# Decay rows stored by unit in device memory, and the Fourier stage's tiles moved to the other side of the on-chip memory

## The chip, the core and the metric

The kernel runs on one core of a Trainium2 chip. The core has a matrix engine (TensorE, PE in the profile; PEld is its weight load), three engines for elementwise work (VectorE or DVE, ScalarE or ACT, GpSimd or POOL), a queue engine (SyncE or SP) that issues nearly all transfers of this kernel, and 16 DMA engines that carry them between device memory (DRAM) and the on-chip memories SBUF and PSUM. Each engine works through its own instructions in order. The metric is the device time of one execution in microseconds; three runs of the kernel before took 3012.8, 3020.76 and 3021.59 us, so the median is 3020.76 us.

## The reference: what is computed

One encoder layer over two sequences (1024 and 2048 tokens of width 1024):

```python
proj = rms_norm(h, norm_w) @ w_in          # z_f, u_f, z_s, xbc, dt for all branches
y_f  = einsum(real(fft2(u_f)), w_fmix) * silu(z_f)            # Fourier branch, 512 wide
x, B, C = silu(conv5(xbc));  dt = softplus(dt_raw + bias)     # SSD branch, 24 heads of 64
# per head and direction, chunks of 128 tokens, a_cs = cumsum(dt * A) inside a chunk:
y_diag = (C B^T * exp(where(mask, a_cs[l] - a_cs[s], -inf))) @ (x * dt)
state  = scan over chunks;   y_off = (C state) * exp(a_cs)
y_s  = rms_norm((y_fwd + y_bwd + D * x) * silu(z_s))
h    = h + concat(y_f, y_s) @ w_out
h    = rms_norm(h + (p @ w_ple_in) * sigmoid(h @ w_ple_gate))
```

The SSD branch runs forward and backward over the tokens; d is the direction (0 forward, 1 backward).

## The kernel before: tiling, stages and order

**Blocks.** The tokens are worked off in three blocks of 1024: P (the short sequence), S1 and S2 (the halves of the long one). Every fp32 product is three matmuls on split operands (high times high, high times low, low times high).

**First stage: projection and SSD.** For each block the normed and turned rows stand in SBUF as `uh`/`ul` (lines 254 to 268). A job (class `Job`) loads 128 columns of `w_in` (`weights_in`, line 182, tile `wr`), splits them (`wh` on ACT, line 189; `wl` on POOL, line 190) and multiplies them in three pieces (line 361). Between those pieces the SSD work of the running units is put. A unit is two heads; there are twelve per block. The order of this stage is written out by hand: `pre` and `post` hang each step of a unit to a numbered slot, and every engine gets its instructions in that order.

**Decay rows.** Once per block `dt_rows` makes `rows` (the cumulated decays `a_cs`, one row of 128 tokens for each of 64 columns and 8 chunks; columns 0 to 23 hold the forward heads, 32 to 55 the backward ones) and `erow`, their exponentials. `dt_out` stores them to `ROWd` and `EXPd`, laid out by chunk, then column, then token. A unit then reads them back spread over the partitions: `rows_in` (line 540, tile `R`, four pairs of chunks, two directions each) for the masked part, `decays` (line 635, tile `er`, two groups of four chunks, two directions and two heads each) for the states' part. `rows_cut` masks `R` on POOL (line 548), `rows_exp` takes the exponential on ACT (558), `rows_joined` adds the two directions and multiplies with `cb` on DVE (563, 564), `diag` multiplies on PE (575) and adds the skip on DVE (580). `weighted` (POOL, 587) and `states` (PE 607, DVE 614 and 618) carry the states; `across` (PE 649, DVE 652 and 653) adds their part with `er`; `gated` (POOL, 658) applies the gate and `out` (line 667) stores `y` to `Yd`.

**Fourier stage.** Behind the first stage, and no longer ordered by hand but by a scheduler that works on a modelled timeline, come eight steps (two sequences, four tiles of channels). Each loads `U` (line 913), folds it into even and odd parts on DVE and POOL (982 to 992), multiplies with small matrices on PE (`pm` 972, `pe` 1000, `pq` 1017), splits (`qh` ACT 1020, `ql` DVE 1021), multiplies with the tables `th`/`tl` (1026) and combines into `yv` (DVE 1030 to 1040, POOL 1044). The tables are loaded through `traw` (928) and split on ACT and DVE (929, 930).

**Products.** Then come the output products (line 1102) in two passes and the last pass with the gated embedding (1292).

**Pools.** SBUF and PSUM are given out as two stacks, one growing from each side. The tiles of the first stage lie in the order `uh`/`ul`, weights, raw tiles, constants, unit tiles, and last the SSD's small tiles with `R`, `er` and `y`. Before, the Fourier stage's inputs, folds and first two tables (`fp`, `ft_`) lie on the right and its outputs and other tables (`fq`, `fc`) on the left, as do `ox`, `wa`, `wb` of the products; in PSUM `pm`/`pe`, `pq` and the first results lie on the right. Tiles of a later pool wait for the tiles of an earlier one whose memory they take over (`reuse_waits="tile"`).

Of the kernel before, what the change touches and what calls it, by code (L numbers as in the profile page):

```python
# [56 lines left out]
def tile_hybrid_encoder(ctx: ExitStack, tc: tile.TileContext, a):  # L57
# [14 lines left out]
    ROWd = [dram.tile([NCH, 64, P], F32, name=f"ROWd{i}") for i in range(3)]  # L72
    EXPd = [dram.tile([NCH, 64, P], F32, name=f"EXPd{i}") for i in range(3)]
# [21 lines left out]
    def bcast_rows(src, n):  # L95
        return src.partition_broadcast(n)
# [5 lines left out]
    with ExitStack() as ph:  # L102
# [63 lines left out]
        def dt_weights_in():  # L166
            wdr = sp.tile([P, KT, 64], F32, tag="R1", bufs=3, name="wdr")
# [70 lines left out]
        def x_normed(b, i, xn):  # L238

            xt, n = xn  # L240
            if b["n"] == "P":
                junk = sp.tile([P, DM], BF16, tag="R0", bufs=3, name="junk")
# [191 lines left out]

        def dt_softplus(B, part):
# [12 lines left out]
            dtm = sp.tile([P, NCH, 64], F32, tag="R1", bufs=3, name="dtm")  # L448
            dmx = sp.tile([P, NCH, 64], F32, tag="R0", bufs=3, name="dmx")
            de = sp.tile([P, NCH, 64], F32, tag="R0", bufs=3, name="de")  # L450
            dz = sp.tile([P, NCH, 64], F32, tag="R1", bufs=3, name="dz")
# [73 lines left out]
        class Unit:  # L525
# [8 lines left out]
            def rows_in(self, p):  # L534
                B, u, cc = self.B, self.u, 2 * p
                self.R[p] = []
                for d in range(2):
                    hc = 32 * d + 2 * u
                    R = sp.tile([P, 2, 2, P], F32, tag=f"R{d}", bufs=3, name=f"R{d}")
                    nc.sync.dma_start(  # L540
                        R.rearrange("p c h l -> p c (h l)"),
                        bcast_rows(ROWd[B.bi][cc:cc + 2, hc:hc + 2, :].rearrange("c h l -> c (h l)"), P))
                    self.R[p].append(R)

            def rows_cut(self, p):
                for d, R in enumerate(self.R[p]):
                    sgn = 1 if d == 0 else -1
                    G.affine_select(  # L548
                        out=R.rearrange("p c h l -> p (c h) l"), in_=R.rearrange("p c h l -> p (c h) l"),
                        pattern=[[0, 4], [sgn, P]], compare_op=ALU.is_ge, fill=NEG, base=0,  # L550
                        channel_multiplier=-sgn)
# [834 lines left out]
```

## Time and profile before

| what | value |
|---|---|
| runs | 3012.8, 3020.76, 3021.59 us |
| the profiled execution's own time | 3021.5 us |
| its span (first to last instruction) | 3019.7 us |
| mean granted TensorE clock | 0.974 |
| busy share PE, PEld, DVE, ACT, POOL | 94%, 85%, 73%, 46%, 49% |
| bytes moved, mean rate | 440.54 MB, 146 GB/s |

The first stage runs to about 1960 us, the Fourier stage from there to about 2100 us, the products to the end. In the profile a line of a timeline gives the start, the time, the engine, the source line, the operation and its tiles, and in square brackets how long the engine had been idle and for what; a line of the stretches gives, for each engine, its busy time and number of instructions, then the granted clock, the busy share of the DMA engines and the rate in GB/s; a line of the waits gives the engine and line that waited, what it waited for, the total, the number of times and the longest.

### The profile page before, as it was taken

The page shows a single profiled execution, that of the slowest core. Times are in us where ns is not written, and L with a number is a line of the kernel's source. Part 1 is how long each engine was busy: PE and PEld are TensorE (multiplying, and loading weights), DVE is VectorE, ACT ScalarE, POOL GpSimd, SP SyncE. Part 2 cuts the span into 40 slices and gives each one's busy share as a digit, 9 for nine tenths or more (in the row PEclk, how much of TensorE's full clock was granted, in tenths as well). Part 3 has the DMA queues.
Part 4 walks back from the last instruction along what each step waited for, and adds up shares of the span by engine and source line. Part 5 has one row for each costly group of instructions (what it writes and reads, how often), then busy time and mean ns, then how long its engine had stood idle before and what let it go on. Part 6 is the DMA issues. An engine that isn't in the chain of part 4 may idle for free. (4 is left out here: it accounts for less than half of the span.)

```text
span 3019.7 us, 47067 instructions
## 1 busy us (share of the span) xinstructions
PE 2831.3 (94%) x17252; PEld 2570.1 (85%) x17252; DVE 2217.9 (73%) x3412; ACT 1389.5 (46%) x2980; POOL 1488.2 (49%) x1114
## 2 busy tenths in 40 slices
PE   6999999989999989989999999978899899989998
PEld 6899999989999889989999999867677677768887
DVE  3687777666778667666868777687989888866665
ACT  4544545434545454434544444334433533355554
POOL 1255646432567566542556564455787688610000
PEclk9999999999999999999999999979999999999999
DMA  3388877872789779853677687666553654352221
GB/s 97 77 130 160 167 156 170 139 142 78 143 163 171 164 188 155 160 153 74 122 164 144 154 160 137 127 217 235 168 181 130 231 166 147 126 199 91 94 85 69
DMA packets 454578, 440.54 MB, mean 146 GB/s; under 512 B 24384, under 2 KB 405444, under 8 KB 450508
## 3 DMA queue, kind: packets, MB, share of 16 engines
q1 hardware_dynamic: 454060, 436.50, 61.5%
q8 instruction: 136, 2.23, 0.3%
q14 instruction: 94, 0.77, 0.1%
q10 hardware_dynamic: 288, 1.05, 0.1%
HBM read 328.41 MB, written 110.10 MB: 145 GB/s over the span
## 5 line engine op out<-in xcount | busy, mean ns | idle before, releaser
L361 PE MATMUL ps<-uh,wh 128*128 128x342 f32 (+1 forms) x2880 | 962.3, 334 | 11.7 <-ACT uh L267 8.5
L361 PE MATMUL ps<-ul,wh 128*128 128x342 f32 (+1 forms) x2880 | 926.1, 322 | 2.5 <-DVE ul L268 2.5
L361 PE MATMUL ps<-uh,wl 128*128 128x342 f32 (+1 forms) x2880 | 927.2, 322 | 0.9 <-POOL wl L190 0.9
L190 POOL TENSOR_TENSOR wl<-wr,wh 128x1024 fp32r<-128x1024 f32 x120 | 298.9, 2491 | 712.2 <-ACT wh L189 698.6
L361 PEld LDWEIGHTS ps<-uh,wh 128*128 128x128 f32 x2880 | 551.2, 191 | 35.3 <-issue 16.0
L361 PEld LDWEIGHTS ps<-ul,wh 128*128 128x128 f32 x2880 | 553.6, 192 | 4.2 <-DVE ul L268 3.5
L361 PEld LDWEIGHTS ps<-uh,wl 128*128 128x128 f32 x2880 | 549.8, 191 | 1.7 <-POOL wl L190 1.6
L558 ACT ACTIVATE R<-R,lb 128x128 f32<-128x128 f32 x1152 | 356.1, 391 | 89.5 <-POOL R L548 88.0
L548 POOL TENSOR_SCALAR_AFFINE_SELECT R<-R 128x512 f32<-128x512 f32 x288 | 270.4, 954 | 117.0 <-DMA R<-ROWd 113.0
L618 DVE SCALAR_TENSOR_TENSOR H<-H,cd,pst 128x64 f32<-128x64 f32 x888 | 182.7, 275 | 92.6 <-PE pst L607 90.4
L587 POOL TENSOR_TENSOR xw<-xm,wd 128x512 f32<-128x512 f32 x144 | 188.6, 1319 | 74.1 <-ACT xm L423 62.5
L1102 PE MATMUL X<-whP,ah 128*128 128x512 f32 x480 | 195.2, 407 | 7.8 <-ACT pu L1111 5.4
L402 DVE SCALAR_TENSOR_TENSOR xT<-raw,cvt,xT 128x1024 f32<-128x1024 f32 x144 | 197.3, 1370 | 2.6
L367 ACT COPY raw<-ps 128x342 f32<-128x342 f32 x180 | 78.3, 438 | 252.9 <-PE ps L361 247.9
L1102 PE MATMUL X<-whP,al 128*128 128x512 f32 x480 | 192.1, 400 | 2.1 <-DVE al L1073 2.1
L1102 PE MATMUL X<-wlP,ah 128*128 128x512 f32 x480 | 193.1, 402 | 0.5 <-DVE wlP L861 0.5
L1214 POOL TENSOR_TENSOR ht<-ht,pu 128x512 f32<-128x512 f32 x96 | 155.4, 1627 | 62.9 <-ACT pu L1111 39.9
L607 PE MATMUL pst<-xw,Bm 128*128 128x128 f32 x1056 | 146.4, 281 | 28.6 <-POOL xw L587 28.6
L607 PEld LDWEIGHTS pst<-xw,Bm 128*128 128x128 f32 x1056 | 137.5, 195 | 33.8 <-POOL xw L587 33.6
L563 DVE TENSOR_TENSOR R<-R,R 128x512 f32<-128x512 f32 x144 | 141.3, 981 | 31.4 <-ACT R L558 28.8
L1073 DVE TENSOR_TENSOR al<-s,ah 128x512 fp32r<-128x512 f32 x144 | 143.6, 1019 | 20.2 <-ACT ah L1072 20.0
L653 DVE TENSOR_TENSOR y<-y,yt 128x512 f32<-128x512 f32 (+1 forms) x144 | 154.6, 1073 | 4.9
(264 smaller groups left out, 5665.4 us busy)
## 6 DMA issues: line engine op xcount, KB each, us to landing
R<-ROWd SPq DMA_DIRECT2D x288, 256.0 KB
wr<-in_w_in SPq DMA_DIRECT2D x120, 512.0 KB
er<-EXPd SPq DMA_DIRECT2D x288, 128.0 KB
Hd<-ht SPq DMA_DIRECT2D x48, 512.0 KB
ht<-Hd SPq DMA_DIRECT2D x48, 512.0 KB
y<-Yd SPq DMA_DIRECT2D x46, 512.0 KB
wlP<-WSd SPq DMA_DIRECT2D x21, 1024.0 KB
Yd<-y SPq DMA_DIRECT2D x72, 256.0 KB
```

Of the source, the lines that this page charges most:

```text
L190: G.tensor_tensor(wl, raw, wh.bitcast(F32), op=ALU.subtract)
L361: T.matmul(ps[:, :n], lhsT=wt[:, kt, :], rhs=ut[:, kt, :n], start=(i == 0), stop=(i == 3 * KT - 1))
L402: V.scalar_tensor_tensor(dst, raw[:, k:k + TB], cvt[:, 20 * k + ct:20 * k + ct + 1], dst, op0=ALU.mult, op1=ALU.add)
L548: G.affine_select(out=R.rearrange("p c h l -> p (c h) l"), in_=R.rearrange("p c h l -> p (c h) l"), pattern=[[0, 4], [sgn, P]], compare_op ...
L558: S.activation(R[:, c, h, :], R[:, c, h, :], AF.Exp, bias=self.B.lb[:, 2 * p + c, hc + h:hc + h + 1])
L587: G.tensor_tensor(xw, self.xm[c4].rearrange("p c (h e) -> p c h e", h=2), col(self.B.wd[:, c4:c4 + 4, hc:hc + 2]).broadcast_to([P, 4, 2, 6 ...
L607: T.matmul(pst[:, c, :], lhsT=B.Bm[self.g][:, c4 + c, :], rhs=xw[:, c, :, :].rearrange("p h e -> p (h e)"), start=True, stop=True)
L618: V.scalar_tensor_tensor(dst[:, e], H[d][:, cc, e], B.cd[:, cc, hc + h:hc + h + 1], pst[:, c, e], op0=ALU.mult, op1=ALU.add)
L653: V.tensor_tensor(y[:, cr], y[:, cr], t[:, cr], op=ALU.add)
L1073: V.tensor_tensor(al, src, ah.bitcast(F32), op=ALU.subtract)
L1102: T.matmul(ps, lhsT=at[:, k, :], rhs=wt[:, k, :], start=(first and i == 0), stop=(i == 11), skip_group_check=not first)
L1214: return lambda t: G.tensor_tensor(h, h, t, op=ALU.add)
```

## The change

**Decay rows.** `ROWd` becomes [pair of chunks, head, direction, 2 x 128] and `EXPd` [group of four chunks, head, direction, 4 x 128]. A unit's rows of one pair, both heads and both directions, stand behind each other, and so do one head's rows of one group in both directions. `rows_in` issues one transfer in place of two, into one tile `R` that holds both directions; `decays` issues two in place of four. `dt_out` stores in four transfers in place of two. The steps on POOL, ACT, DVE and PE work on the same numbers with other strides. The tiles `R0` and `R1` (three buffers each) become one tag `R` of twice the size with three buffers, which the constants and the softplus use too.

**Pools.** All pools behind the first stage change sides; in PSUM `pm`/`pe` and `pq` come to the left and all results `pr` to the right.

```diff
-    ROWd = [dram.tile([NCH, 64, P], F32, name=f"ROWd{i}") for i in range(3)]
-    EXPd = [dram.tile([NCH, 64, P], F32, name=f"EXPd{i}") for i in range(3)]
+    ROWd = [dram.tile([4, 24, 2, 2 * P], F32, name=f"ROWd{i}") for i in range(3)]
+    EXPd = [dram.tile([2, 24, 2, 4 * P], F32, name=f"EXPd{i}") for i in range(3)]
...
+        def pair_of(name):
+            t = sp.tile([P, 2, NCH, 64], F32, tag="R", bufs=3, name=name)
+            return t[:, 0], t[:, 1]
...
-            nc.sync.dma_start(ROWd[B.bi].rearrange("c h l -> h c l"), B.rows)
-            nc.sync.dma_start(EXPd[B.bi].rearrange("c h l -> h c l"), B.erow)
+            for d in range(2):
+                for kept, src, n in ((ROWd, B.rows, 2), (EXPd, B.erow, 4)):
+                    nc.sync.dma_start(kept[B.bi][:, :, d, :].rearrange("p h x -> h p x"),
+                                      src[32 * d:32 * d + 24].rearrange("h (p c) l -> h p (c l)", c=n))
...
             def rows_in(self, p):
-                B, u, cc = self.B, self.u, 2 * p
-                self.R[p] = []
-                for d in range(2):
-                    hc = 32 * d + 2 * u
-                    R = sp.tile([P, 2, 2, P], F32, tag=f"R{d}", bufs=3, name=f"R{d}")
-                    nc.sync.dma_start(
-                        R.rearrange("p c h l -> p c (h l)"),
-                        bcast_rows(ROWd[B.bi][cc:cc + 2, hc:hc + 2, :].rearrange("c h l -> c (h l)"), P))
-                    self.R[p].append(R)
+                R = sp.tile([P, 2, 2, 2, P], F32, tag="R", bufs=3, name="R")
+                nc.sync.dma_start(
+                    R.rearrange("p h d c l -> p (h d c l)"),
+                    bcast_rows(ROWd[self.B.bi][p, 2 * self.u:2 * self.u + 2].rearrange("h d x -> (h d x)"), P))
+                self.R[p] = R
...
-                V.tensor_tensor(E[0], E[0],
-                                self.B.cb[self.g][:, 2 * p:2 * p + 2, :].unsqueeze(2).broadcast_to([P, 2, 2, P]),
-                                op=ALU.mult)
+                cb = self.B.cb[self.g][:, 2 * p:2 * p + 2, :].rearrange("p c l -> p (c l)")
+                V.tensor_tensor(E[0], E[0], cb.unsqueeze(1).broadcast_to([P, 2, 2 * P]), op=ALU.mult)
...
-            def decays(self, d, c4):
+            def decays(self, c4):
-                hc = 32 * d + 2 * self.u
-                er = sp.tile([P, 4, P], F32, tag=f"er{d}", bufs=2, name=f"er{d}")
+                er = sp.tile([P, 2, 4, P], F32, tag="er", bufs=2, name="er")
                 for h in range(2):
-                    nc.sync.dma_start(er[h * 64:h * 64 + 64],
-                                      bcast_rows(EXPd[self.B.bi][c4:c4 + 4, hc + h, :], 64))
-                self.er[d, c4] = er
+                    nc.sync.dma_start(
+                        er[h * 64:h * 64 + 64].rearrange("p d c l -> p (d c l)"),
+                        bcast_rows(EXPd[self.B.bi][c4 // 4, 2 * self.u + h].rearrange("d x -> (d x)"), 64))
+                self.er[c4] = er
...
-    ox = ctx.enter_context(tc.tile_pool(name="ox", bufs=1, **L_))
-    wa = ctx.enter_context(tc.tile_pool(name="wa", bufs=1, **L_))
+    ox = ctx.enter_context(tc.tile_pool(name="ox", bufs=1, **R_))
+    wa = ctx.enter_context(tc.tile_pool(name="wa", bufs=1, **R_))
...
-        ft_ = ph.enter_context(tc.tile_pool(name="ft_", bufs=1, **R_))
-        fp = ph.enter_context(tc.tile_pool(name="fp", bufs=2, **R_))
-        fq = ph.enter_context(tc.tile_pool(name="fq", bufs=2, **L_))
-        fc = ph.enter_context(tc.tile_pool(name="fc", bufs=1, **L_))
+        ft_ = ph.enter_context(tc.tile_pool(name="ft_", bufs=1, **L_))
+        fp = ph.enter_context(tc.tile_pool(name="fp", bufs=2, **L_))
+        fc = ph.enter_context(tc.tile_pool(name="fc", bufs=1, **R_))
+        fq = ph.enter_context(tc.tile_pool(name="fq", bufs=2, **R_))
+        fpl = ph.enter_context(tc.tile_pool(name="fpl", bufs=1, space=PSUM, **L_))
         fpr = ph.enter_context(tc.tile_pool(name="fpr", bufs=1, space=PSUM, **R_))
-        fpl = ph.enter_context(tc.tile_pool(name="fpl", bufs=1, space=PSUM, **L_))
...
-            pm = fpr.tile([P, 2, P], F32, tag="pm", name="pm")
+            pm = fpl.tile([P, 2, P], F32, tag="pm", name="pm")
...
-                pr = (fpr if i < 2 else fpl).tile([P, 512], F32, tag="pr", bufs=2 + i // 2, name="pr")
+                pr = fpr.tile([P, 512], F32, tag=f"pr{i // 2}", bufs=2 + i // 2, name="pr")
...
-    mp = ctx.enter_context(tc.tile_pool(name="mp", bufs=1, **R_))
+    mp = ctx.enter_context(tc.tile_pool(name="mp", bufs=1, **L_))
...
-                    q4 = ctx.enter_context(tc.tile_pool(name="q4", bufs=1, **R_))
+                    q4 = ctx.enter_context(tc.tile_pool(name="q4", bufs=1, **L_))
```

**How instructions move.** The lines of the changed kernel are one or two lower than the same lines before. A number behind a name counts tiles and says nothing here; what stands behind the arrow is read.

SP in the first unit of block P, before: loads of the rows `R` and `er` between those of the weights `wr`.

```order
L182 DMA wr<-in_w_in 128x8x128
L540 DMA R_1112<-ROWd_67 128x2x256
L540 DMA R_1114<-ROWd_67 128x2x256
L182 DMA wr<-in_w_in 128x8x128
L540 DMA R_1225<-ROWd_67 128x2x256
L540 DMA R_1227<-ROWd_67 128x2x256
L635 DMA er_1272<-EXPd_70 64x4x128 x2
L635 DMA er_1275<-EXPd_70 64x4x128 x2
L182 DMA wr<-in_w_in 128x8x128
L635 DMA er_1386<-EXPd_70 64x4x128 x2
L635 DMA er_1389<-EXPd_70 64x4x128 x2
```

The same place in the changed kernel.

```order
L182 DMA wr<-in_w_in 128x8x128
L540 DMA R<-ROWd_67 128x1024
L182 DMA wr<-in_w_in 128x8x128
L540 DMA R<-ROWd_67 128x1024
L633 DMA er<-EXPd_70 64x1024 x2
L182 DMA wr<-in_w_in 128x8x128
L633 DMA er<-EXPd_70 64x1024 x2
```

Nothing changes its place; each pair of `R` has become one transfer and each four of `er` two, with 1024 numbers in a row.

SP at the end of the first stage, before: the last unit's loads of `er`, the stores of the last projections (`UFd`, `ZFd`), of a state (`HBd`) and of the last unit's output (`Yd`), and then the Fourier stage's first inputs (`bd`, `U`, `wbd`).

```order
L667 DMA Yd_62<-y 128x512
L635 DMA er_20600<-EXPd_72 64x4x128 x2
L635 DMA er_20603<-EXPd_72 64x4x128 x2
L288 DMA UFd_64<-ft 128x1024
L635 DMA er_20679<-EXPd_72 64x4x128 x2
L635 DMA er_20682<-EXPd_72 64x4x128 x2
L979 DMA Z<-ZFd_65 128x1024
L288 DMA ZFd_66<-ft 128x1024
L288 DMA HBd<-hend 128x128
L667 DMA Yd_62<-y 128x512 x2
L900 DMA bd<-in_bdft 128x2x128
L913 DMA U<-UFd_63 128x1024
```

The same place in the changed kernel.

```order
L666 DMA Yd_62<-y 128x512
L633 DMA er<-EXPd_72 64x1024 x2
L288 DMA UFd_64<-ft 128x1024
L633 DMA er<-EXPd_72 64x1024 x2
L898 DMA bd<-in_bdft 128x2x128
L911 DMA U<-UFd_63 128x1024
L905 DMA wbd<-in_w_fmix 64x4x64
L288 DMA ZFd_66<-ft 128x1024
L905 DMA wbd<-in_w_fmix 64x4x64
L926 DMA traw<-in_tabs 128x512 x2
L911 DMA U<-UFd_63 128x1024 x2
L926 DMA traw<-in_tabs 128x512 x2
```

`bd` and `U` now stand right behind the last `er`; the two stores of `Yd` have gone behind the loads of `U` and `traw`, and the first `Z` too.

PE at the same place, before: the last unit's masked part (`pd`) and states' part (`po`), then the Fourier stage's first products.

```order
L575 MATMUL pd<-R_20447,xm 64x128 x4
L649 MATMUL po_20702<-CT,H_20584 128x128 x4
L649 MATMUL po_20710<-CT,H_20523 128x128 x4
L575 MATMUL pd<-R_20554,xm 64x128 x4
L649 MATMUL po_20725<-CT,H_20584 128x128 x3
L649 MATMUL po_20732<-CT,H_20523 128x128 x4
L972 MATMUL pm<-wbd,bd 128x128 x2
L1000 MATMUL pe<-edge,mt 128x2
```

The same place in the changed kernel.

```order
L574 MATMUL pd<-R,xm 64x128 x4
L970 MATMUL pm<-wbd,bd 128x128 x2
L998 MATMUL pe<-edge,mt 128x2
L1015 MATMUL pq<-mt,fold_20330 128x128 x2
L1015 MATMUL pq<-mt,fold_20331 128x128 x2
L648 MATMUL po_20198<-CT,H_20086 128x128 x4
L648 MATMUL po_20206<-CT,H_20027 128x128 x4
L574 MATMUL pd<-R,xm 64x128 x4
L648 MATMUL po_20221<-CT,H_20086 128x128 x3
L648 MATMUL po_20228<-CT,H_20027 128x128 x4
```

The first step's `pm`, `pe` and `pq` now stand ahead of the last unit's `po` and its last `pd`. DVE and POOL are mixed in the same way: DVE's first fold of `U` (line 980 of the changed kernel) stands between the addition and the multiplication of the last unit's third `R`.

More of the change, by code (lines that the diff above doesn't have):

```diff
@@ L534, in rows_in, with rows_cut @@
             def rows_in(self, p):
[L535 to L546 removed]
+                R = sp.tile([P, 2, 2, 2, P], F32, tag="R", bufs=3, name="R")
[3 more added lines that the diff above has]
+                self.R[p] = R
+            def rows_cut(self, p):
+                for d in range(2):
+                    R = self.R[p][:, :, d]
                     sgn = 1 if d == 0 else -1
[L548 to L551, printed above, removed]
+                    G.affine_select(out=R, in_=R, pattern=[[0, 2], [0, 2], [sgn, P]], compare_op=ALU.is_ge, fill=NEG,
+                                    base=0, channel_multiplier=-sgn)
             def rows_exp(self, p):
[L554 removed]
+                R = self.R[p]
+                for d in range(2):
                     hc = 32 * d + 2 * self.u
@@ L576, in diag @@
                                  lhsT=self.xm[c4][:, c2 + c, h * 64:h * 64 + 64],
-                                 rhs=self.R[p][0][:, c, h, :], start=True, stop=True)
+                                 rhs=self.R[p][:, h, 0, c, :], start=True, stop=True)
                 if p % 2:
@@ L690, in plan @@
                 post(s0 + 12, self.states, 1, 0)
-                for d in (1, 0):
-                    pre(s0 + 11, self.decays, d, 0)
-                    pre(s0 + 13, self.decays, d, 4)
+                pre(s0 + 11, self.decays, 0)
+                pre(s0 + 13, self.decays, 4)
                 for p in range(4):
```

31 lines of the change are left out of this document (14 added, 17 removed).

## The prediction

> **What bounds the kernel now.** I read the engines' busy shares first, then the stretches by stage, then PE's waits and the timeline around the longest. The busy shares and five stretches (start to end, busy time and instructions of each engine, granted clock, DMA share, GB/s):
>
> ```profile
> PE 2831.3 (94%) x17252; PEld 2570.1 (85%) x17252; DVE 2217.9 (73%) x3412; ACT 1389.5 (46%) x2980; POOL 1488.2 (49%) x1114
> ...
> 30.00:1950.00 1920.00, 1843.08 (x12778) 1779.54 (x12777) 1372.71 (x2320) 905.15 (x2044) 992.48 (x764) 0.98 0.72 142
> 1950.00:1975.50 25.50, 7.35 (x54) 6.45 (x54) 12.85 (x34) 1.50 (x5) 3.68 (x4) 0.70 0.66 173
> 1975.50:2060.00 84.50, 69.84 (x349) 60.59 (x349) 81.21 (x158) 38.59 (x97) 51.21 (x30) 0.84 0.67 235
> 2060.00:2100.00 40.00, 40.00 (x195) 33.75 (x196) 22.40 (x35) 14.12 (x24) 18.94 (x13) 0.92 0.43 155
> ```
>
> PE sets the time, so only what PE loses can be won. In the first stage (30 to 1950 us) it is idle for 1920 - 1843.08 = 76.9 us and granted 0.98 of its clock, another 38 us at most (0.02 x 1920, partly the same idle time). In the 25.5 us behind it PE works 7.35 us: a hole between two stages. Then DVE is the bound (81.21 of 84.5 us) with PE at 0.84 of its clock, and then PE again (40 of 40 us). Who kept PE, POOL, DVE and ACT waiting (total us, times, longest):
>
> ```profile
> PE pst L607 <- POOL xw L587: 28.6, 18, 6.9
> PE pt L264 <- DVE xt L250: 20.8, 5, 12.2
> PE pm L972 <- DVE Ue L985: 15.8, 1, 15.8
> PE pt L264 <- DVE H L618: 13.6, 4, 5.6
> ...
> POOL R L548 <- DMA R<-ROWd: 113.0, 57, 4.7
> ...
> DVE xt L250 <- DMA xt<-in_x_sample: 27.9, 4, 12.4
> ...
> ACT wh L189 <- DMA wr<-in_w_in: 56.2, 31, 6.2
> ```
>
> The 12.2 us is the kernel's start, which nothing here touches. The 15.8 us is the hole. Behind the others stand transfers. The timeline of all engines shows two such stalls, at the start of block S1 and inside it:
>
> ```profile
> 634.92 11.02 SPq L122 DMA_DIRECT2D xt<-in_x_sample  x1
> 646.52 1.28 DVE L250 SCALAR_TENSOR_TENSOR xt<-xt,ss,nwb 114x1024 f32<-114x1024 f32 x1 [12.42 <-DMA xt<-in_x_sample]
> 647.96 1.82 PE L264 MATMUL pt<-ident,xt 114*128 114x114 f32 x8 [5.72 <-DVE xt L250]
> ...
> 1118.24 2.35 POOL L190 TENSOR_TENSOR wl<-wr,wh 128x1024 fp32r<-128x1024 f32 x1 [4.47 <-ACT wh L189]
> 1125.24 2.08 PE L607 MATMUL pst<-xw,Bm 128*128 128x128 f32 x8 [6.88 <-POOL xw L587]
> ```
>
> In the first DVE stands 12.42 us for `xt`, whose issue on SP took 11.02 us, and PE loses 5.72 us. In the second POOL is late with `wl`, because `wh` and before it the load `wr` were late, and `xw` queues behind. The hole itself:
>
> ```profile
> 1940.04 0.87 SPq L540 DMA_DIRECT2D R<-ROWd  x2
> 1946.13 7.45 SPq L635 DMA_DIRECT2D er<-EXPd  x4
> 1961.61 7.56 SPq L667 DMA_DIRECT2D Yd<-y  x2
> 1969.74 0.46 SPq L913 DMA_DIRECT2D U<-UFd  x1
> ...
> 1948.24 0.32 PE L361 MATMUL ps<-uh,wl 128*128 128x342 f32 x1
> 1949.82 0.63 POOL L548 TENSOR_SCALAR_AFFINE_SELECT R<-R 128x512 f32<-128x512 f32 x1 [3.21 <-DMA R<-ROWd]
> ...
> 1964.83 0.56 DVE L652 TENSOR_TENSOR yt<-po,er 128x384 f32<-128x384 f32 x1 [3.94 <-DMA er<-EXPd]
> 1967.57 1.26 POOL L658 TENSOR_TENSOR y<-y,zT 128x512 f32<-128x512 f32 x1 [5.98 <-DVE y L653]
> 1974.67 0.69 DVE L982 TENSOR_TENSOR Ue<-U 128x511 f32<-128x511 f32 x1 [3.65 <-DMA U<-UFd]
> 1975.50 1.20 PE L972 MATMUL pm<-wbd,bd 128*128 128x128 f32 x4 [15.76 <-DVE Ue L985]
> ```
>
> The last four `er` loads take SP 7.45 us to issue and land at 1964.83; `y` is gated at 1967.57; SP holds its queue 7.56 us for the stores of `y`; only then `U` is issued, 21 us after the last projection (1948.24), and PE starts 15.76 us after it ran dry.
>
> **The change part by part.** *Instructions.* PE, ACT, DVE and POOL keep their counts and element counts. The steps concerned (us in all, mean ns):
>
> ```profile
> L558 ACT ACTIVATE R<-R,lb 128x128 f32<-128x128 f32 x1152 | 356.1, 391 | 89.5 <-POOL R L548 88.0 <-DMA wr<-in_w_in 1.4
> L548 POOL TENSOR_SCALAR_AFFINE_SELECT R<-R 128x512 f32<-128x512 f32 x288 | 270.4, 954 | 117.0 <-DMA R<-ROWd 113.0 <-DVE yt L652 4.0
> L563 DVE TENSOR_TENSOR R<-R,R 128x512 f32<-128x512 f32 x144 | 141.3, 981 | 31.4 <-ACT R L558 28.8 <-issue 2.4
> ```
>
> Their operands become two runs of 256 numbers instead of one of 512. No row has that form; the masks in the row above already ran as four rows of 128, so I take 0. If each of the 288 masks and 288 additions and multiplications on DVE cost 50 ns more, that is 14 us on engines with 928 and 547 us of idle time in the first stage: still under 2 us on PE.
>
> *Transfers.* 288 loads `R` become 144, 288 loads `er` become 144; six stores are added (4 for 2 in each of three blocks), under the projections of the first unit. How the DMA engines carry short and long runs (the queue's totals, the two tables' loads, and three stretches of 10 us):
>
> ```profile
> q1 hardware_dynamic: 454060, 436.50, 61.5%
> R<-ROWd SPq DMA_DIRECT2D x288, 256.0 KB
> er<-EXPd SPq DMA_DIRECT2D x288, 128.0 KB
> 630.00:640.00 10.00, 10.00 (x74) 9.62 (x73) 3.98 (x5) 3.94 (x11) 4.16 (x6) 1.00 1.03 76
> 640.00:650.00 10.00, 4.28 (x26) 3.89 (x25) 3.35 (x5) 1.75 (x4) 1.04 (x2) 0.81 0.67 177
> 2040.00:2050.00 10.00, 8.72 (x50) 7.23 (x48) 10.00 (x17) 8.30 (x16) 2.80 (x2) 1.00 1.02 399
> ```
>
> A load `R` reads runs of two heads by 128 numbers, 1 KB, so 256 runs each; a load `er` runs of 512 B, also 256. That is 2 x 73728 of the queue's 454060 packets. Afterwards both read runs of 4 KB: 144 x 128 + 144 x 64 = 27648. The bytes stay. If time goes with bytes, the share stays 61.5%; if it goes with packets, it falls to 61.5% x 334/454 = 45%. The nearest rows: the crowded stretch from 630 us carries 76 GB/s with the engines full, the Fourier stage's, whose loads have long runs, 399 GB/s. The first stage's mean, 142 GB/s at 0.72, is 197 GB/s at a full share. The two tables' 113 MB (288 x 384 KB) take 574 us of full engines at 197 GB/s and 284 us at 399: 290 us less, 9.6% of the span. So I take a share of about 50%, between the two bounds.
>
> What PE wins: the waits above that a late transfer can end are, without the start, 5.7 + 13.6 + 28.6 = 48 us, with up to 38 us of clock behind all 77. Bounds: 0 and 86 us. I take three quarters of the waits at the block starts (`xt` late: 14 us), a quarter of the waits for `xw` (POOL also waits there for other things: 8 us) and a sixth of the clock (6 us): **28 us**.
>
> *The hole.* `U` can be issued when the last projection has read `uh` and `ul` (1948.24 + 0.32) and lands 4.93 us later, as before (1969.74 to 1974.67): 1953.5. In the changed order nothing but the `er` loads and two stores stands ahead of it on SP. DVE then fills its idle time in the hole, 25.5 - 12.85 = 12.65 us, less some 2 us in which the first folds pass from engine to engine: 10.6 us. PE, which starts earlier and without the long pause behind which its clock was 0.84, gives about 3 us more in the stretch to 2100, where it is the bound at clock 0.92. Sum **14 us**. Bound above: DVE's work from 1950 to 2100 is 12.85 + 81.21 + 22.4 = 116.5 of 150 us, so 33 us. Bound below: 0, if the mixing costs what it wins: DVE's first fold waits for `U` ahead of the third `R`'s multiplication, `pd` queues behind that on PE, and PE's `po` behind `pe` and `pq`. With `U` at 1953.5 that holds `pd` until about 1955 and PE idles some 4 us; each us by which `U` comes later is a us lost.
>
> The stores `Yd` and the load `Z`, now behind `U` on SP, are read in the products and at the end of a Fourier step; the Fourier stage covers them. Should `Z` be late, POOL's gate of `yv` is late next.
>
> Against the profiled execution's own 3021.5 us: 3021.5 - 28 - 14 = 2979.5; the median lies 0.7 us under it, so **2979 us**.
>
> **The rivals.** (1) *Run length does not matter.* For it stands the stretch from 640 us above: 177 GB/s at 0.67 is 264 at a full share, with the same tables' loads in it, so the 76 is an extreme, and what keeps 399 away may be the spreading of one row over many partitions, which stays. Against it stands the first stage's mean, half of 399. Then the first stage keeps its stalls: 3021 - 14 = 3007. The Trainium skill has a rule to that effect: "DMA: Bandwidth & Descriptors", Specifications, calls 512 B the smallest transfer at line rate. By it both tables' runs are long enough already, and the sum would be 3007. The rows above do not bear it out for this traffic.
>
> (2) *The hole's time comes back.* DVE bounds the Fourier stage, and its order there is another; if folds and table splits now hold `pr` up, only the first stage's gain and 2 us stay: 2991.
>
> (3) *Slower: the first mask waits for both directions.* Today the two halves of `R` land apart: the last pair was issued at 1940.04 and the second mask still waited 3.21 us at 1949.82. In one transfer the first mask gets nothing before the whole has landed, and POOL's `xw` queues behind it. POOL's 113 us of waiting for `R` go with PE's 28.6 us for `xw`, a quarter. If every one of 144 first masks came x us later than now, PE would lose 36x us. Without the gain of 28 us and with that of the hole, it is slower by more than 9 us from x = 0.64; at x = 1 it gives 3021 - 14 + 36 = 3043. Against it: fewer packets should bring the whole sooner than the second half came.
>
> (4) *It does little.* The stalls stem from SP's order and POOL's load rather than from the engines' load, and the hole is half closed: about 3014.
>
> **How the numbers follow.** Forecast 62%, rival (1) 14%, (2) 12%, (3) 5%, (4) 7%. The forecast's own range is 2958 to 2999: 10 to 45 us from the first stage, 8 to 25 from the hole, seldom both at an end. With (1) and (2) the range is **2956 to 3008**. A change of 0.3% (9 us) can be told from none: faster by more than that are the forecast, (2) and most of (1), 0.87; the same (4) and the rest of (1), 0.08; slower (3), 0.05.
>
> **What would show it.** In the profile of the changed kernel: POOL's wait for `R` well under 113 us and the queue's share near 50%; no 12 us wait of DVE for `xt`; PE idle in the first stage some 50 us instead of 77 at clock 0.99. `U` issued before 1950 us less the gain so far, and no PE gap over 5 us between the last projection and `pm`. Wrong: a share near 61% with the same waits (rival 1), DVE idle in the Fourier stage and PE waiting for `ql` and folds (2), POOL's wait for `R` above 113 us (3).

## The result

The changed kernel takes 2939.93 us (median, 2936.23 to 2940.29) against 3018.89 us of the kernel before (3012.8 to 3021.59, with a fourth run beside the three named at the start): a ratio of 0.974, 95% interval 0.972 to 0.976. It is some 79 us faster; forecast were 42, and 2939.9 lies below the range of 2956 to 3008 us.

The profile page of the changed kernel, its busy shares and its largest DMA queue (packets, MB, share of the 16 engines):

```profile
PE 2803.6 (95%) x17252; PEld 2549.2 (87%) x17252; DVE 2218.9 (76%) x3412; ACT 1384.3 (47%) x2980; POOL 1513.5 (52%) x1114
...
q1 hardware_dynamic: 327484, 436.08, 47.0%
```

Nearly the same bytes (436.08 MB, 436.50 before) kept the queue busy for 47.0% of 2937.6 us instead of 61.5% of 3019.7 us, which is 1381 instead of 1857 us of full engines. To place the gain I cut both executions at the same two points, the end of the last projection on PE and the start of the first output product. The kernel before by these stretches (start to end and length; busy time of PE, PEld, DVE, ACT, POOL; clock, DMA share, GB/s):

```profile
30.00:1948.56 1918.56, 1841.64 (x12764) 1778.39 (x12763) 1371.80 (x2316) 903.75 (x2039) 992.30 (x763) 0.98 0.72 142
1948.56:2097.40 148.84, 116.04 (x601) 99.88 (x600) 115.08 (x225) 54.01 (x128) 72.54 (x45) 0.84 0.60 204
2097.40:3019.70 922.30, 860.86 (x3837) 680.44 (x3836) 719.41 (x849) 415.86 (x787) 417.94 (x298) 0.98 0.42 144
```

The changed kernel by the same view:

```profile
30.00:1868.95 1838.95, 1813.63 (x12757) 1755.52 (x12756) 1377.61 (x2320) 896.32 (x2038) 1019.89 (x765) 1.00 0.49 149
1868.95:2007.30 138.35, 112.64 (x602) 97.45 (x601) 113.89 (x223) 56.10 (x130) 71.04 (x44) 0.88 0.60 209
2007.30:2937.60 930.30, 864.56 (x3837) 684.97 (x3835) 716.17 (x848) 415.77 (x785) 417.28 (x298) 0.98 0.42 143
```

The first stage is 79.6 us shorter (1918.56 - 1838.95). PE's idle time there fell from 76.9 to 25.3 us, which is 51.6 us, and nearly the same matmuls (12757 records for 12764) took 28.0 us less busy time, at clock 1.00 instead of 0.98. The stretch up to the first product lost 10.5 us, the products grew by 8.0. So nearly all of the net gain, 79.6 of 82.1 us, is the first stage's.

PE's, POOL's and ACT's waits in the changed kernel (total us, times, longest):

```profile
POOL R L549 <- DMA R<-ROWd: 6.8, 3, 3.9
...
PE pt L264 <- DVE xt L250: 14.5, 3, 12.2
...
ACT wh L189 <- DMA wr<-in_w_in: 4.7, 2, 4.2
PE pst L606 <- POOL xw L586: 3.4, 9, 0.9
...
PE pt L264 <- DVE H L617: 2.6, 2, 2.0
```

POOL waits 6.8 us for `R` instead of 113.0, ACT 4.7 us for `wr` instead of 56.2, PE 3.4 us for `xw` instead of 28.6. The 14.5 us for `xt` all lie in the first 30 us, the kernel's start. The loads of `R` now leave SP almost at once. How long SP held the issue of a load `R`, kernel before (shortest/median/longest in ns, first and last start in us):

```profile
L540 SPq DMA_DIRECT2D R<-ROWd x288: 359/546/7210, 119.2 to 1940.5; - x144
```

The changed kernel:

```profile
L540 SPq DMA_DIRECT2D R<-ROWd x144: 319/327/836, 118.9 to 1860.6; - x144
```

Its timeline at the start of block S1, where SP's issue of `xt` had taken 11.02 us, and through the transition:

```profile
603.60 0.69 SPq L122 DMA_DIRECT2D xt<-in_x_sample  x2
...
1868.80 0.32 PE L361 MATMUL ps<-uh,wl 128*128 128x342 f32 x1
...
1869.14 0.33 SPq L911 DMA_DIRECT2D U<-UFd  x1
...
1873.59 0.69 DVE L980 TENSOR_TENSOR Ue<-U 128x511 f32<-128x511 f32 x1 [1.02 <-DMA U<-UFd]
...
1876.21 1.12 PE L574 MATMUL pd<-R,xm 128*64 128x128 f32 x8 [4.75 <-DVE H L617]
...
1877.26 1.23 PE L970 MATMUL pm<-wbd,bd 128*128 128x128 f32 x4
...
1893.55 1.22 PE L970 MATMUL pm<-wbd,bd 128*128 128x128 f32 x4 [6.91 <-DVE ed L1000]
```

`U` is issued when the last projection has read its operands, and `pm` stands 8.5 us behind that projection instead of 27.3. A new gap of 6.91 us follows ahead of the second step's `pm`.

### The profile page after: what moved, and what is told of

It is laid out like the page before. It is cut to its first block, busy times and chain, and to the rows that moved or that the text cites. A ratio compares the mean times of both kernels' runs of the same rounds, so it can differ in the third digit from the quotient of the medians.

```text
span 2937.6 us, 46491 instructions
## 1 busy us (share of the span) xinstructions
PE 2803.6 (95%) x17252; PEld 2549.2 (87%) x17252; DVE 2218.9 (76%) x3412; ACT 1384.3 (47%) x2980; POOL 1513.5 (52%) x1114
## 3 DMA queue, kind: packets, MB, share of 16 engines
q1 hardware_dynamic: 327484, 436.08, 47.0%
## 5 line engine op out<-in xcount | busy, mean ns | idle before, releaser
L361 PEld LDWEIGHTS ps<-uh,wh 128*128 128x128 f32 x2880 | 544.4, 189 | 36.3 <-issue 15.6
L361 PEld LDWEIGHTS ps<-ul,wh 128*128 128x128 f32 x2880 | 547.3, 190 | 4.2 <-DVE ul L268 3.5
L361 PEld LDWEIGHTS ps<-uh,wl 128*128 128x128 f32 x2880 | 543.7, 189 | 1.2 <-POOL wl L190 0.9
L1100 PE MATMUL X<-whP,ah 128*128 128x512 f32 x480 | 196.3, 409 | 15.9 <-ACT pu L1109 12.4
L1212 POOL TENSOR_TENSOR ht<-ht,pu 128x512 f32<-128x512 f32 x96 | 155.7, 1631 | 64.4 <-ACT pu L1109 49.9
L652 DVE TENSOR_TENSOR y<-y,yt 128x512 f32<-128x512 f32 (+1 forms) x144 | 161.3, 1120 | 4.9
L565 DVE TENSOR_TENSOR R<-R,cb 128x512 f32<-128x512 f32 x144 | 149.7, 1040 | 4.9
L272 ACT ACTIVATE zT<-ps 128x342 f32<-128x342 f32 (+1 forms) x108 | 49.1, 454 | 220.7 <-PE ps L361 220.4
L651 DVE TENSOR_TENSOR yt<-po,er 128x512 f32<-128x512 f32 (+1 forms) x144 | 91.2, 633 | 74.9 <-PE po L648 66.9
```

What stands on the lines that cost most here:

```text
L361: T.matmul(ps[:, :n], lhsT=wt[:, kt, :], rhs=ut[:, kt, :n], start=(i == 0), stop=(i == 3 * KT - 1))
L565: V.tensor_tensor(E[0], E[0], cb.unsqueeze(1).broadcast_to([P, 2, 2 * P]), op=ALU.mult)
L652: V.tensor_tensor(y[:, cr], y[:, cr], t[:, cr], op=ALU.add)
L1100: T.matmul(ps, lhsT=at[:, k, :], rhs=wt[:, k, :], start=(first and i == 0), stop=(i == 11), skip_group_check=not first)
L1212: return lambda t: G.tensor_tensor(h, h, t, op=ALU.add)
```

## The experiments

My theory was the prediction's: long runs, so fewer packets. The rivals were the number of transfers, and that the pools' sides had brought the gain. Ratios are against runs of the kernel before beside it on the same chip (medians from 3012.6 to 3018.65 us).

**The two halves of the change.** The first kernel has the rows alone, the second the pools' sides alone.

```diff
 # e1_rows: the changed kernel, and for all pools behind the first stage
-    ox = ctx.enter_context(tc.tile_pool(name="ox", bufs=1, **R_))
+    ox = ctx.enter_context(tc.tile_pool(name="ox", bufs=1, **L_))
...
 # e2_sides: the kernel before, and for all those pools
-    ox = ctx.enter_context(tc.tile_pool(name="ox", bufs=1, **L_))
+    ox = ctx.enter_context(tc.tile_pool(name="ox", bufs=1, **R_))
```

> The decay rows alone; the pools behind the first stage stay on their old sides. In the changed kernel the last projection on PE starts 79 us earlier than before (1868.8 for 1948.2 us), the stretch from there to the first output product is 10 us shorter and the products are 8 us longer. Theory A (the first stage's gain is all of it and comes from the rows): last projection near 1869 us, time 2935 to 2950 us. Theory B (the gain needs the other sides, since the Fourier stage's inputs come in earlier): last projection later than 1900 us, time above 2970 us. If the 10 us and the 8 us belong to the sides, the stretch behind the last projection is about 149 us and the products about 922 us, as before.

> The pools' sides alone; the decay rows as before. Theory A: the first stage is as before (last projection near 1948 us), time 3005 to 3020 us; by the prediction's term for the hole (14 us) it is 3005, by what the two traces show behind the last projection (10 us less, 8 us more) it is 3017. Theory B: 2990 us or less. If the longer products come from the sides, they take about 930 us here too.

The rows alone: 2937.44 us, ratio 0.974 (0.972 to 0.976). The sides alone: 3025.96 us, ratio 1.003 (1.002 to 1.005), so a little slower, outside what either theory had said for them. Theory A holds for the first stage: the whole gain is the rows'. The rows alone by the same stretches:

```profile
30.00:1871.10 1841.10, 1817.07 (x12766) 1758.90 (x12765) 1377.26 (x2316) 897.25 (x2040) 1020.36 (x765) 1.00 0.49 149
1871.10:2014.40 143.30, 112.96 (x603) 97.14 (x602) 115.10 (x225) 54.27 (x128) 71.87 (x44) 0.88 0.57 202
2014.40:2935.60 921.20, 860.49 (x3837) 681.49 (x3835) 718.95 (x849) 415.49 (x786) 418.35 (x298) 0.98 0.43 144
```

Of the 10.5 us behind the last projection the rows bring 5.5 without any change of sides (148.84 to 143.30); `U` is issued 16.4 us behind the last projection there, before it was 21.5. With the sides alone `U` comes late, and everything mixed with it waits. SP's, DVE's and PE's rows of that kernel at this place:

```profile
1946.42 7.26 SPq L635 DMA_DIRECT2D er<-EXPd  x4
1953.73 2.57 SPq L900 DMA_DIRECT2D bd<-in_bdft  x1
1956.40 2.77 SPq L913 DMA_DIRECT2D U<-UFd  x1
...
1967.95 0.69 DVE L982 TENSOR_TENSOR Ue<-U 128x511 f32<-128x511 f32 x1 [15.55 <-DMA U<-UFd]
...
1970.57 1.12 PE L575 MATMUL pd<-R,xm 128*64 128x128 f32 x8 [19.27 <-DVE H L618]
```

The old, slow loads `er` and `bd` behind them hold SP until 1956.3. The first fold, which stands among the last unit's steps on DVE, waits 15.55 us for `U`, and the last unit's `pd` stands behind it: PE idles 19.27 us in one piece. The fold starts 19.3 us behind the last projection (1948.63) here and 4.8 us behind it in the changed kernel; the difference of 14.5 us is also that of PE's two gaps (19.27 and 4.75). The products take 926.7 us, 4.4 more than before; some 930 were expected if the sides make them longer.

**Run length against number of transfers.** One kernel has the changed order of the rows, with gaps behind the runs: short runs, few transfers. The other has long runs in as many transfers as before.

```diff
 # e3_gaps: the changed kernel with 64 numbers of gap behind each run
-    ROWd = [dram.tile([4, 24, 2, 2 * P], F32, name=f"ROWd{i}") for i in range(3)]
-    EXPd = [dram.tile([2, 24, 2, 4 * P], F32, name=f"EXPd{i}") for i in range(3)]
+    ROWd = [dram.tile([4, 24, 2, 2 * P + 64], F32, name=f"ROWd{i}") for i in range(3)]
+    EXPd = [dram.tile([2, 24, 2, 4, P + 64], F32, name=f"EXPd{i}") for i in range(3)]
...
 # e4_split: the changed kernel, each load R in two (and er likewise in pieces of 32 partitions)
+                for e in (0, 64):
-                nc.sync.dma_start(
-                    R.rearrange("p h d c l -> p (h d c l)"),
-                    bcast_rows(ROWd[self.B.bi][p, 2 * self.u:2 * self.u + 2].rearrange("h d x -> (h d x)"), P))
+                    nc.sync.dma_start(
+                        R[e:e + 64].rearrange("p h d c l -> p (h d c l)"),
+                        bcast_rows(ROWd[self.B.bi][p, 2 * self.u:2 * self.u + 2].rearrange("h d x -> (h d x)"), 64))
```

> The changed kernel with a gap of 64 numbers behind each run in device memory: R is read in runs of 1 KB and er in runs of 512 B, as before the change, by the same 144 + 144 transfers of the same bytes as after it. Theory A1 (the length of the runs, so the number of packets): the DMA share goes back to about 61%, POOL's wait for R to about 100 us, the last projection to about 1945 us, time 3010 to 3020 us. Theory A2 (fewer transfers, so less issuing on SP and fewer transfers under way): no change against the changed kernel, 2940 us, share 47%.

> The changed kernel with the long runs of 4 KB, but as many transfers as before the change: each load R is two transfers of 64 partitions and each pair of er loads four of 32 partitions. Theory A1 (length of runs): share 47%, last projection near 1869 us, time 2937 to 2945 us. Theory A2 (number of transfers): the gain is lost, 3010 to 3020 us.

Gaps: 2939.41 us, 0.975 (0.973 to 0.977). Split: 2938.56 us, 0.975 (0.973 to 0.977). Both keep the whole gain, and my theory falls; fewer transfers are not needed either. The kernel with gaps, its largest queue:

```profile
q1 hardware_dynamic: 448228, 436.08, 49.1%
```

Its POOL's wait for `R`:

```profile
POOL R L550 <- DMA R<-ROWd: 7.7, 3, 4.1
```

It has nearly as many packets as before (448228 for 454060) of the same sizes, and a share of 49.1%. Between gaps and no gaps (327484 packets, 47.0%) lie 2.1 points; between the kernel before and the one with gaps lie 12.4. So a packet was not dear because it was short. The split kernel's share is 49.3% with 332092 packets, where 47% was expected; its time does not show it. That long runs or few transfers are each enough alone is not excluded by these two kernels, but by one of the next three, which has neither. What the two share and the kernel before lacks is the place of the runs in device memory: those of a load `R` within 5 KB and those of a load `er` within 6, where before they stood a chunk's 64 rows apart, 64 x 512 B = 32 KB.

**The distance of the runs.** Three kernels tell the distance from the number of different runs in a load (four in a load `R` after the change, two before) and from their nearness.

```diff
 # f1_stride: the kernel before with 66 rows for each chunk: runs 33 KB apart
-    ROWd = [dram.tile([NCH, 64, P], F32, name=f"ROWd{i}") for i in range(3)]
-    EXPd = [dram.tile([NCH, 64, P], F32, name=f"EXPd{i}") for i in range(3)]
+    ROWd = [dram.tile([NCH, 66, P], F32, name=f"ROWd{i}") for i in range(3)]
+    EXPd = [dram.tile([NCH, 66, P], F32, name=f"EXPd{i}") for i in range(3)]
...
 # f2_merge: the changed kernel with the tables as before, one load for both directions
+                    bcast_rows(ROWd[self.B.bi][2 * p:2 * p + 2].rearrange("c (d h) l -> (c d) (h l)", d=2)
+                               [:, 2 * self.u * P:(2 * self.u + 2) * P], P))
...
 # f3_two: the kernel with gaps, with one load for each direction as before
+                for d in range(2):
+                    nc.sync.dma_start(
+                        R[:, :, d].rearrange("p h c l -> p h (c l)"),
+                        bcast_rows(ROWd[self.B.bi][p, 2 * self.u:2 * self.u + 2, d, 0:2 * P], P))
```

> The kernel before with 66 instead of 64 rows for each chunk in both decay tables, so that the runs of one load stand 33 KB apart instead of 32 KB; the same loads, the same runs of 1 KB and 512 B, the same number of transfers and packets (454 thousand). The runs with gaps and with split transfers both kept the whole gain, so neither the length of runs nor the number of transfers makes it. Theory S (the distance of 32 KB, a power of two, between the runs of one load slows the reads): share near 50%, POOL's wait for R near 8 us, the last projection near 1871 us, time 2935 to 2950 us. Theory H (it is the number of different runs that one load spreads over the 16 engines: two in a load R before, four after) and theory F (the runs of a load must lie close together): no change against before, 3010 to 3025 us.

> The changed kernel with the decay tables laid out as before (runs of a load 16 and 32 KB apart), but both directions in one transfer: 144 + 144 loads, each R of four runs of 1 KB, each er of eight runs of 512 B, for every partition. Theory S and theory F: slow as before, last projection near 1946 us, share near 61%, 3010 to 3025 us. Theory H: fast, 2935 to 2950 us.

> The changed kernel with gaps (runs of 1 KB and 512 B that lie within 5 KB) and with the loads cut as before the change: two transfers R of two runs, four transfers er of four runs. So lengths, number of runs and number of transfers are all as before, and only the place of the runs is new. Theory S and theory F: the gain stays, 2935 to 2950 us, share near 50%. Theory H: it goes, 3010 to 3025 us.

With 66 rows: 2938.29 us, 0.975 (0.972 to 0.977): two sizes in the declarations of the kernel before (and the slices of its stores that go with them) bring the whole gain. Its largest queue:

```profile
q1 hardware_dynamic: 454060, 436.50, 49.9%
```

Its POOL's wait for `R`:

```profile
POOL R L548 <- DMA R<-ROWd: 9.1, 6, 2.4
```

The packets are those of the kernel before to the last one, and the share is 49.9% instead of 61.5%. The two stores of each block change their distance too, but they are 1.6 of the 436.5 MB. The third kernel has short runs and as many loads as before, and only the place is new: 2940.36 us, 0.975 (0.973 to 0.978). Its largest queue:

```profile
q1 hardware_dynamic: 452836, 436.10, 48.5%
```

Theory H falls, and so does nearness (F), since 33 KB is far. The merged loads on the old tables are slower than before, 3104.97 us, 1.030 (1.027 to 1.033). Their largest queue:

```profile
q1 hardware_dynamic: 449452, 436.48, 60.3%
```

Their waits on POOL and PE:

```profile
POOL R L548 <- DMA R<-ROWd: 171.4, 65, 8.4
...
PE pst L605 <- POOL xw L585: 69.5, 33, 5.2
```

The queue is busy for 60.3% of 3103.6 us, 1871 us, hardly more than before (1857). But POOL waits 171.4 us instead of 113.0 and PE 69.5 us for `xw` instead of 28.6. In one transfer the first mask waits for both directions; that this makes the longer waits is my reading, and the runs do not show it by itself.

**Which distances.** Four kernels are like the one with 66 rows but with 72, 80, 88 and 96; one has 66 rows in `ROWd` alone.

```diff
 # g_72: (g_80, h_88, g_96: 80, 88, 96; g_rowd: 66 in ROWd, 64 in EXPd)
-    ROWd = [dram.tile([NCH, 66, P], F32, name=f"ROWd{i}") for i in range(3)]
-    EXPd = [dram.tile([NCH, 66, P], F32, name=f"EXPd{i}") for i in range(3)]
+    ROWd = [dram.tile([NCH, 72, P], F32, name=f"ROWd{i}") for i in range(3)]
+    EXPd = [dram.tile([NCH, 72, P], F32, name=f"EXPd{i}") for i in range(3)]
```

> As the kernel with 66 rows, with 72 rows for each chunk: the runs of a load stand 36 KB apart, an odd multiple of 4 KB. Theory S1 (only distances that are multiples of a large power of two, 16 or 32 KB, are slow): 2935 to 2950 us, share near 50%. Theory S2 (the runs must differ in a lower part of the address, within 4 KB): slow as before, 3005 to 3025 us, share near 61%.

> The same with 96 rows: the runs stand 48 KB apart, an odd multiple of 16 KB; four runs of er then fall on two places modulo 32 KB. Theory S1 with 32 KB as the distance that matters: R fast and er half slow, 2940 to 2975 us. Theory S1 with 16 KB or less: slow as before, 3005 to 3025 us.

> As the kernel with 66 rows, but for ROWd alone; the runs of er stay 32 KB apart. If the two tables share the loss by what their packets cost too much (by the shares of the whole, R's reads the larger part): share near 53 to 56%, POOL's wait for R 10 to 40 us, time 2945 to 2985 us. If the reads of er alone are enough to crowd the queue: 2990 us or more.

> As the kernel with 66 rows, with 80 rows for each chunk: the runs stand 40 KB apart, an odd multiple of 8 KB. So far 33 and 36 KB gave 2938 and 2937 us, 48 KB 2993 us, 32 KB 3017 us; with ROWd alone at 33 KB it was 2943 us, so the 48 KB must slow R itself. If the loss grows with the power of two in the distance: between the two, 2940 to 2985 us. If only multiples of 16 KB are slow: 2935 to 2945 us, as with 36 KB.

> As the kernel with 66 rows, with 88 rows for each chunk: the runs stand 44 KB apart, an odd multiple of 4 KB. If multiples of 8 KB are slow and odd multiples of 4 KB are not (36 KB gave 2937 us, 40 KB 3004 us): 2933 to 2947 us, share near 51%. If the loss depends on the distance in another way, for example on what lies between 36 and 48 KB: 2960 to 3010 us.

The kernels with 72, 88 and 96 rows and with 66 in `ROWd` alone have two runs each, the one with 80 has six.

| distance of the runs | kernel | us | ratio (95%) | share of q1 |
|---|---|---|---|---|
| 32 KB | before | 3018.89 | 1 | 61.5% |
| 33 KB | 66 rows | 2938.29 | 0.975 (0.972 to 0.977) | 49.9% |
| 36 KB | 72 rows | 2937.04 | 0.973 (0.971 to 0.975) | 51.2% |
| 40 KB | 80 rows | 3004.20 | 0.996 (0.994 to 0.999) | 60.8% |
| 44 KB | 88 rows | 2936.01 | 0.974 (0.971 to 0.977) | 51.6% |
| 48 KB | 96 rows | 2992.71 | 0.992 (0.990 to 0.994) | 59.2% |
| 33 KB, `er` 32 KB | 66 rows in `ROWd` | 2942.77 | 0.975 (0.973 to 0.978) | 50.8% |

The largest queues at 40 and at 44 KB:

```profile
q1 hardware_dynamic: 454060, 436.50, 60.8%
```

```profile
q1 hardware_dynamic: 454060, 436.50, 51.6%
```

36 KB is fast, so S2 falls. Three expectations of this series missed. 48 KB came between its two ranges, 40 KB above both of its own: the loss does not simply grow with the power of two in the distance. What the series shows is simpler: the three multiples of 8 KB are slow, and the three other distances are fast. This guess, made from the first five, gave 2933 to 2947 us for 44 KB, and 2936.01 came. The three are not equally slow. Of some 80 us, 40 KB wins back 14 and 48 KB 24 (POOL's wait for `R` is 107.4 and 64.6 us); between those two the intervals touch. The size of the tables is no rival: the changed kernel's, at 192 KB each, are a multiple of 64 KB like the slow ones (256, 320 and 384 KB), and are quick.

The third miss is the kernel with 66 rows in `ROWd` alone: it came below all that was said for it, with POOL's wait at 9.0 us. Of the two tables `ROWd` carries the loss. With `er` still at 32 KB the share is 50.8%, against 49.9% with both moved, and the times cannot be told apart. A kernel with `EXPd` alone moved was not run.

**The merging again.**

```diff
 # h_merge33: the kernel f2_merge with 33 rows for each direction: runs 16.5 KB apart
-    ROWd = [dram.tile([NCH, 64, P], F32, name=f"ROWd{i}") for i in range(3)]
-    EXPd = [dram.tile([NCH, 64, P], F32, name=f"EXPd{i}") for i in range(3)]
+    ROWd = [dram.tile([NCH, 2, 33, P], F32, name=f"ROWd{i}") for i in range(3)]
+    EXPd = [dram.tile([NCH, 2, 33, P], F32, name=f"EXPd{i}") for i in range(3)]
```

> The kernel with the old layout and both directions in one transfer (3105 us), with 33 instead of 32 rows for each direction: the four runs of a load R and the eight of a load er now stand 16.5 KB apart instead of 16 KB. Theory D (distance alone makes it slow; the merging only shows it up, since the first mask then waits for both directions' slow reads): fast, 2935 to 2950 us, POOL's wait for R under 15 us. Theory M (the merging over distant runs is slow by itself): 3000 us or more.

2939.30 us, 0.975 (0.973 to 0.977). POOL's wait for `R` in this kernel:

```profile
POOL R L549 <- DMA R<-ROWd: 12.7, 3, 5.6
```

Theory D holds: the merging costs nothing where the reads are quick. Where they are slow, the merged kernel took 92 us more than the kernel before (3012.6 us beside it). It has the new sides too, which alone cost 0.3%, some 10 us; its first stage, from 30 us to the last projection, is 71 us longer than that of the sides alone (1990.0 and 1918.6). How much of this is the first mask's waiting and how much that four and eight runs, 16 KB apart, meet in one transfer instead of two and four was not told apart.

**Other tables.**

```diff
 # g_pads: the changed kernel
-    Yd = [dram.tile([P, 16, TB], F32, name=f"Yd{i}") for i in range(3)]
+    Yd = [dram.tile([P, 17, TB], F32, name=f"Yd{i}") for i in range(3)]
 # and likewise one more in UFd, ZFd, ZSd, CTd
```

> The changed kernel with one more row in the middle dimension of the other tables in device memory (Yd, UFd, ZFd, ZSd, CTd), so that the partitions' runs stand 68, 20 or 40, 52 and 20 KB apart instead of 64, 16 or 32, 48 and 16 KB. Each of their runs is read or written once by one partition, not 64 or 128 times. If the distance slows those too: the stretch from the last projection to the end gets shorter by 10 us or more, 2905 to 2932 us. If only rows read many times over suffer: no change, 2936 to 2944 us.

2939.16 us, 0.974 (0.972 to 0.976): no change, and a share of 47.1% for 47.0%. In this kernel the tables of which each run is read once had nothing to win.

**The sides, once the rows are right.** The kernel with the rows alone and the changed kernel as they are, side by side on one chip.

> The decay rows alone, in five rounds beside the changed kernel on the same chip. If the sides cost what they cost alone (0.3%, 9 us): 5 to 10 us faster than the changed kernel. If the two stretches of the profiles cancel: within 4 us of it.

> The changed kernel again, beside the kernel with the rows alone: 2937 to 2943 us. If the prediction's term for the hole held (14 us from the sides), it would be 10 us or more faster than the rows alone.

2939.32 us for the rows alone, ratio 0.974 (0.972 to 0.975), and 2940.11 us for the changed kernel, 0.974 (0.973 to 0.976): the sides are worth nothing that can be measured; the 5 to 10 us that they cost alone do not show here, nor do the 14 of the prediction. The profiles agree with the first two of these kernels. From the start of the last projection to the first product it is 143.4 and 143.3 us with the rows alone and 138.5 and 138.8 with the sides; from there to the end 921.2 and 924.9 against 930.3 and 927.1. What the sides take out of the transition (4.9 and 4.5 us) stands again in the products (9.1 and 2.2 us). All other profiles bear this out: from the first product to the end nine profiles with the old sides take 919.3 to 924.9 us, and nine with the new ones 926.4 to 930.3. Why the products are longer I have not tested.

No version beat the changed kernel by more than can be measured.

## Why the prediction missed

The direction was right; the size was not, and the mechanism was wrong. Three things failed: what makes a transfer dear, the shares of each wait and of the clock in the first stage's 28 us, and the worth of the sides in the hole's 14 us. The miss in size is the second's. The gain itself was in part luck, as the new layout happens to bring near each other the runs whose distance was the price.

**The price of the transfers.** The step "if it goes with packets, it falls to 61.5% x 334/454 = 45%" rested on the rates of stretches with short and with long runs. It never asked what else set those apart. The share came out at 47.0%, near the 50% taken, but by luck and by another cause: with all the packets kept, it is 49.9%. Rival (1) was right that run length does not matter here, and wrong that the stalls would then stay (3007 us): it shared my assumption that nothing else about the reads had changed. The diff had it in sight: old runs a chunk apart, `[NCH, 64, P]`, new ones side by side.

The prediction weighed one rule of the Trainium skill, that 512 B is the smallest transfer at line rate ("DMA: Bandwidth & Descriptors", Specifications). It held that the rows did not bear this out, and that was a misreading: the kernel with gaps agrees with the rule, since its runs of 512 B and 1 KB cost 2.1 points of share and no time. The same page of the Trainium skill has a row that I passed over: in "Latency and other measured facts" it says that copies whose rows lie large powers of two apart run slower, and that 4 KB more between the rows brings the full rate back, 192 B not. It measured distances from 512 KB up, with rows that one partition reads. Here 32 KB was enough, for rows that 128 partitions read, and 1 KB more cured it; 40 and 48 KB, which are no powers of two, were slow as well.

**The first stage: 28 us forecast, 79.6 measured**, near the bound of 86. The waits and their bound were named rightly; the fractions taken of them were too small, and that is the term of the sum that failed.
- The block starts, forecast 14 us: PE's waits for `xt` behind the kernel's start and for `H` went from 5.7 + 13.6 to 0 + 2.6 us, 16.7 us. Nearly right.
- `xw`, forecast a quarter of 28.6, 8 us (7 by its own numbers): 25.2 us went. "POOL also waits there for other things" was the wrong step. The other things (`wh` from `wr`, 56.2 to 4.7 us) were late for the same reason.
- Other waits of PE, not in the sum: the idle time fell by 51.6 us in all, so nearly 10 us more.
- The clock, forecast a sixth, 6 us: 28.0 us of busy time went. I took the 0.98 as mostly a thing of its own. It went with the stalls: in every kernel with quick reads it is 0.99 or 1.00 over this stage, with 23.7 to 27.8 us of idle time on PE, and in the slowest kernel, with 131.8 us, 0.98.

**The hole: 14 us forecast.** The steps came as written: `U` issued at the end of the last projection, `pd` held 4.75 us (forecast some 4), `pm` early. The stretch gave 10.5 us. But 5.5 of them are the rows', whose loads let SP go sooner, and what the sides add comes back in the products, so that the sides' part of the term is nothing that can be measured. Rival (2) named this in kind, in another place: the time came back behind the Fourier stage. The condition "each us by which `U` comes later is a us lost" is borne out with the sides alone: the first fold is 14.5 us later, and PE's gap 14.5 us longer.

**Rival (3)** fits what happened where the reads are slow, though the cause was not told apart there: the merged loads on the old tables took 92 us more than the kernel before, some 10 of them for the sides. Its counterargument, "fewer packets should bring the whole sooner", held in outcome and not in reason.

**Strides on the engines, taken at 0:** the masks took 973 ns on average instead of 954, the additions on DVE 974 instead of 981 and the multiplications 1040 instead of 1050. Right.

## What to carry to other kernels

Before blaming the length of runs or the number of transfers, look at how far apart in device memory the runs lie that one transfer reads, above all where many partitions read the same rows: change the distance a little (here by two rows in a declaration; in this case any distance tried that was no multiple of 8 KB did) and measure. If the DMA share falls at the same bytes, packets and transfers, place was the price. And when a shared resource is what makes transfers late, do not give each wait a fraction of its own: here nearly all of them, and the clock behind them, went together.

## What the runs showed of the hardware

Reads of rows that 128 partitions take (`R`, runs of 1 KB) were slow where the runs of one transfer stood 32, 40 or 48 KB apart (shares of the queue 61.5, 60.8 and 59.2%) and quick at 33, 36 and 44 KB (49.9 to 51.6%), with equal bytes and packets. For rows that 64 partitions take (`er`, runs of 512 B) 32 KB alone cost nothing that can be measured (50.8% for 49.9%). Which part of the memory they meet in, and why 48 KB loses less than 32 KB, stays open. The slowness also fell on transfers that had nothing to do with these tables: SP was held by a load `xt` for 0.80 us in the median and 11.02 at the longest with 32 KB, and for 0.37 and 1.99 us with 33 KB (66 rows).
